# A hybrid decoder layer with dense experts: more blocks of first expert products between and ahead of the top-16 selection, the one-hot stage and the second products

## The chip, the cores and the metric

One core of one Trainium2 chip runs the whole layer. The metric is device microseconds of one execution of the program; lower is better. The engines are named as the profile names them: PE (TensorE matmul), PEld (its weight loads), DVE (VectorE), ACT (ScalarE), POOL (GpSimd), SP (SyncE, which here only issues DMAs). Matrix operands are split into a rounded part and a remainder ("hi" and "lo") and multiplied in three passes.

## The reference

```python
h2  = modulate(rms_norm(x, norm2_g), shift2, scale2)      # after conv, attention and w_out
q   = (h2 @ w_peer_q).reshape(T, 8, 2, 128)
s1, s2 = q[:, :, 0] @ keys1.T, q[:, :, 1] @ keys2.T        # 8 heads, 128 + 128 keys
v1, i1 = top_k(s1, 16);  v2, i2 = top_k(s2, 16)
cand   = v1[..., :, None] + v2[..., None, :]               # 256 sums, index i1 * 128 + i2
top_s, top_p = top_k(cand, 16);  g = softmax(top_s)
a = einsum('thkd,td->thk', expert_u[idx], h2)              # 16384 experts of one neuron
w = gelu(a) * g
ffn = einsum('thk,thkd->td', w, expert_v[idx])
x = x + gate2 * ffn
```

There are 512 tokens, 2048 features, 128 x 128 experts, all float32.

## The kernel before

The front part (modulation, projections, attention, output projection, query projection `w_peer_q`) is not touched. The expert part treats two groups of tokens differently. The first TG = 160 tokens gather their chosen experts' rows by indirect DMA on POOL's queue and combine them on DVE (`gather_u`, `gather_v`: 320 gathers of 1 MB in 323 steps). The other TD = 352 tokens are done densely: every expert is multiplied with every token, and a table of gates, zero for experts that were not chosen, picks out the result.

The dense part runs over NK = 128 blocks of 128 experts. A **first product** (`u_block(e)`) is 48 matmuls of 352 columns into a PSUM tile `pa`. Its weights come as 1 MB `ur` from `u_dram`; each half of a block is turned by a DVE transpose (blocks 12 and up), split by ACT (hi) and by DVE (lo, `ut<-ur,ut`, in `split`) into `ut`, of which there are two buffers, so that the split of half n + 1 can stand ahead of the matmuls of half n. GELU writes the result to a tile of `GE`. `w_block(e)` multiplies a pair of results with the gates `g` from `g_dram` and splits them into a `W` tile (five buffers). A **second product** (`v_group(ch, dg)`) is 96 matmuls over a chunk of CH = 8 blocks, with weights `vr` split into `vs`; sixteen chunks of four groups. `u_dram` is the first expert matrix laid out in blocks, by copies from DRAM to DRAM (`lay_out`, four DMAs of 256 KB per block, on SP's queue, 116 blocks in all) that are spread over the whole front part.

Between the query projection and the chunks stand two stages. The **last selection**: for each of the four tiles of 128 tokens `select(i, 3, ...)` does the top-16 work of the last two heads, nearly all on DVE (`top16`; `tkj` compares on DVE, multiplies on POOL, reduces on DVE to `idxf`), and `finish_select` the softmax and the transposes of indices and gates (`fi`, `opT`). The **one-hot stage**: in 11 rounds of 32 tokens, four steps each, DVE writes one-hot rows (`gt<-iof,opT`, 128x2048), POOL and ACT scale them to `og`, PE multiplies them (`pv<-og,gt`, 8 matmuls a step), ACT collects `gtile`, and a DMA stores 2 MB of gates to `g_dram`. The first gates can be loaded only after the last store has landed.

RUN = 12 first products are done ahead of the chunks: four before the four tiles of the last selection, eight after the last eight one-hot rounds. Their results wait in two W tiles (blocks 0 to 7) and in `gacc` (8 to 11), an accumulator that the gathers of the second kind need later.

Every engine runs its instructions in program order; the order is made by a scheduler from the order of the code, the data and the extra orderings that the code adds (`add_manual_dep` with ORDER). SP's DMAs are issued in its program order too. The steps of the gathers are tied to `pace`, a list of matmuls.

## Time and profile before

| | |
|---|---|
| median of 3 runs | 3346.73 us (3344.19 to 3349.19) |
| profiled execution | 3349.88 us, of which 3347.6 us span |
| mean granted TensorE clock | 0.978 of full speed |
| PE busy | 3176.0 us, 95% of the span |
| DVE busy | 2739.1 us, 82% |
| ACT, POOL busy | 1223.3 us (37%), 1057.7 us (32%) |
| DMA | 1017.81 MB, 304 GB/s on the mean |

The expert part begins near 1180 us with the first of the 48 x 128 first-product matmuls; the last selection lies between 1185 and 1257 us, the one-hot stage between 1264 and 1400 us, and the second products begin at 1416 us. From there to 3250 us the chunks run, and the last 100 us add the gathered part and store the output. A row of the trace gives the start or a count, then the busy time, and in brackets or behind the bar the idle time ahead of it and what ended it.

### The profile page before, as it was taken

Reading aid. Unit: us, or ns where it says so; the run is one execution under the profiler, and the core shown is the slowest. Engines: PE = TensorE matmul, PEld = TensorE weight load, DVE = VectorE, ACT = ScalarE, POOL = GpSimd, SP = SyncE. Lnnn points to the kernel's source line nnn. Section 1 sums busy time; section 2 is a strip of 40 time slices with the busy share of each in tenths; the row PEclk is TensorE's granted clock in tenths of the full one; section 3 lists DMA queues with packets and bytes.
Section 4 is the critical chain, followed back from the end, with each engine's and each line's share of the span. In section 5 each row is a group of like instructions: output and inputs, shape, how many; then the busy total and the mean of one; then the engine's idle time right before and its main releaser. Section 6 shows DMA issues by size and latency. Waiting matters only on the chain.

```text
span 3347.6 us, 47029 instructions
## 1 busy us (share of the span) xinstructions
PE 3176.0 (95%) x18006; PEld 2945.2 (88%) x18006; DVE 2739.1 (82%) x3631; ACT 1223.3 (37%) x1866; POOL 1057.7 (32%) x709
## 2 busy tenths in 40 slices
PE   5889999999999859999999999999999999999998
PEld 4777877777777659999999999999999999999997
DVE  6888477842338998789999899999999999999975
ACT  5246343343255336632333333333333333333322
POOL 2447333353435634312222232222222222222210
PEclk9999999999999979999999999999999999999998
DMA  9878978966979878989989899998988898999964
GB/s 303 283 257 294 345 250 280 299 211 221 315 256 302 261 243 288 335 290 364 343 332 343 310 333 363 325 338 323 340 333 316 336 354 329 360 330 338 338 222 158
DMA packets 388896, 1017.81 MB, mean 304 GB/s; under 512 B 29713, under 2 KB 108478, under 8 KB 328126
## 3 DMA queue, kind: packets, MB, share of 16 engines
q1 hardware_dynamic: 342590, 679.23, 59.8%
q0 software_dynamic: 46080, 335.56, 25.7%
q8 instruction: 141, 2.31, 0.3%
q14 instruction: 85, 0.70, 0.1%
HBM read 965.11 MB, written 171.18 MB: 339 GB/s over the span
## 4 chain that ended last, share of the span: by engine, by line
PE 55%; DVE 4%; issue 2%; DMA 1%; ACT 0%; POOL 0%; DVEq 0%; ACTq 0%; SPq 0%; POOLq 0%
PE pa L835 26%; PE pv L1004 26%; PE pv L974 2%; DVE gacc L910 1%; DVE ut L90 1%; DMA xs<-x_dram 1%; DVE gt L963 1%; DVE ur L823 1%; DVE vs L90 1%; DMA gt<-in_expert_v_dram,idxu 0%; DMA gt<-in_expert_u_dram,idxu 0%; ACT ut L89 0%; DVE acc L1020 0%; PE pv L1061 0%; DVE gt L897 0%
## 5 line engine op out<-in xcount | busy, mean ns | idle before, releaser
L835 PE MATMUL pa<-hd,ut 128*128 128x352 f32 x6144 | 1067.2, 326 | 37.5 <-DVE ut L90 23.6
L1004 PE MATMUL pv<-W,vs 128*128 128x352 f32 x6144 | 1052.1, 325 | 5.1 <-ACT W L89 2.6
L835 PEld LDWEIGHTS pa<-hd,ut 128*128 128x128 f32 x6144 | 1010.9, 190 | 42.4 <-DVE ut L90 26.6
L1004 PEld LDWEIGHTS pv<-W,vs 128*128 128x128 f32 x6144 | 1001.8, 189 | 8.0 <-ACT W L89 3.5
L90 POOL TENSOR_TENSOR wsp<-wraw,wsp 128x1024 fp32r<-128x1024 f32 x160 | 389.0, 2434 | 557.6 <-ACT wsp L89 525.4
L89 ACT ACTIVATE vs<-vr 128x1024 fp32r<-128x1024 f32 x256 | 271.6, 1061 | 737.9 <-PE pv L1004 687.8
L89 ACT ACTIVATE ut<-ur 128x1024 fp32r<-128x1024 f32 x256 | 269.6, 1056 | 315.2 <-PE pa L835 239.5
L897 DVE SCALAR_TENSOR_TENSOR gt<-gt,h2n 128x2048 f32<-128x2048 f32 x160 | 364.6, 2283 | 18.3 <-DMA gt<-in_expert_u_dram,idxu 18.3
L910 DVE SCALAR_TENSOR_TENSOR gacc<-gt,ga_a,gacc 128x2048 f32<-128x2048 f32 x158 | 369.9, 2341 | 6.8 <-DMA gt<-in_expert_v_dram,idxu 6.7
L889 POOL DMA_INDIRECT gt<-in_expert_u_dram,idxu x128 | 183.0, 1430 | 554.6 <-DVE gt L897 320.8
L90 DVE TENSOR_TENSOR vs<-vr,vs 128x1024 fp32r<-128x1024 f32 x256 | 311.2, 1216 | 57.3 <-ACT vs L89 56.9
L90 DVE TENSOR_TENSOR ut<-ur,ut 128x1024 fp32r<-128x1024 f32 x256 | 310.9, 1219 | 55.6 <-ACT ut L89 54.4
L889 POOL DMA_INDIRECT gt<-in_expert_v_dram,idxu x128 | 172.4, 1347 | 552.3 <-DVE gacc L910 360.1
L89 ACT ACTIVATE wsp<-wraw 128x1024 fp32r<-128x1024 f32 x160 | 169.2, 1058 | 346.5 <-issue 72.0
L507 PE MATMUL pm<-big,wsp 128*128 128x512 f32 x1152 | 285.2, 401 | 0.0
L823 DVE STREAM_TRANSPOSE ur<-ur 128x1024 f32<-128x1024 f32 x232 | 274.5, 1221 | 0.1
L507 PEld LDWEIGHTS pm<-big,wsp 128*128 128x128 f32 x1152 | 214.9, 191 | 42.6
L282 PE MATMUL pqk<-wsp,big 128*128 128x512 f32 x768 | 190.1, 407 | 18.0 <-DVE qk L334 13.6
L748 PE MATMUL pm<-big,wsp 128*128 128x512 f32 x768 | 188.5, 403 | 19.0 <-POOL wsp L90 17.4
L282 PEld LDWEIGHTS pqk<-wsp,big 128*128 128x128 f32 x768 | 148.7, 196 | 53.0 <-DVE qk L334 17.0
L748 PEld LDWEIGHTS pm<-big,wsp 128*128 128x128 f32 x768 | 147.2, 195 | 52.2 <-POOL wsp L90 20.0
L593 PE MATMUL pm<-big,wsp 128*128 128x512 f32 x768 | 182.1, 397 | 6.2 <-DVE x L599 6.2
(274 smaller groups left out, 3024.0 us busy)
## 6 DMA issues: line engine op xcount, KB each, us to landing
ur<-u_dram SPq DMA_DIRECT2D x128, 1024.0 KB, 7.8
vr<-in_expert_v_dram SPq DMA_DIRECT2D x256, 512.0 KB, 7.2
u_dram<-in_expert_u_dram SPq DMA_DIRECT2D x464, 256.0 KB, 6.7
ada_w<-in_w_ada_dram SPq DMA_DIRECT2D x192, 512.0 KB, 5.5
wraw<-in_w_in_dram SPq DMA_DIRECT2D x96, 512.0 KB, 5.7
g_dram<-gtile SPq DMA_DIRECT2D x11, 2048.0 KB, 7.4
g<-g_dram SPq DMA_DIRECT2D x32, 704.0 KB, 9.4
wraw<-in_w_out_dram SPq DMA_DIRECT2D x32, 512.0 KB, 5.5
```

Source lines behind the costliest of these rows:

```text
L89: hi = nc.scalar.activation(dst[:, 0], src, AF.Copy)
L90: (eng or nc.vector).tensor_tensor(out=dst[:, 1], in0=src, in1=dst[:, 0].bitcast(F32), op=OP.subtract)
L282: nc.tensor.matmul(banks[i], hT[kk][:, a, i * P:(i + 1) * P], ws[:, b, k], start=(kk == last[0] and n == 0), stop=(kk == last[1] and n == 2))
L507: nc.tensor.matmul(banks[n2], ws[:, a, k, n2 * P:(n2 + 1) * P], hT[kk][:, b], start=(kk == 0 and n == 0), stop=(kk == KC - 1 and n == 2))
L593: nc.tensor.matmul(banks[j], ws[:, a, k, j * P:(j + 1) * P], yT[kk0 + k][:, b], start=(kq == 0 and k == 0 and n == 0), stop=(kq == 7 and k ...
L748: nc.tensor.matmul(banks[j], ws[:, a, k, j * P:(j + 1) * P], h2T[kk][:, b], start=(kk == 0 and n == 0), stop=(kk == KC - 1 and n == 2))
L823: nc.vector.transpose(t, t)
L835: mm = nc.tensor.matmul(pa[:, :TD], ut[:, a, j].rearrange("p b r -> p (b r)"), hd[k][:, b], start=(k == 0 and n == 0), stop=(k == KC - 1 a ...
L889: d = nc.gpsimd.indirect_dma_start(out=t, out_offset=None, in_=src, in_offset=bass.IndirectOffsetOnAxis(ap=gidx[g][:, j:j + 1], axis=0))
L897: return lambda: nc.vector.scalar_tensor_tensor(t, t, 1.0, h2n, op0=OP.mult, op1=OP.mult, accum_out=ga_a[:, j:j + 1])
L910: return lambda: nc.vector.scalar_tensor_tensor(gacc, t, a, gacc, op0=OP.mult, op1=OP.add)
L1004: mm = nc.tensor.matmul(pv[j // 2][:, j % 2, :TD], vs[:, a, bb, j * P:(j + 1) * P], W[e0 // 2][:, m, bb], start=(b == 0 and n == 0), stop= ...
```

## The change

The change moves work in time and adds a detour by DRAM; no product, selection or gather is added or dropped.

- RUN becomes 16. `u_block` becomes a generator of halves (`u_halves`), so that `u_half(upto)` can do one half (24 matmuls) at a time.
- In the last selection `select` calls `between()` after each of its portions; `one_more` there does one half of a block and ties the next portion's first DVE instruction behind that half's lo split (`after[0] = split.lo`). Ten blocks (RUN_TK) are done so, where before there were four.
- The other six go into the one-hot stage, spread over its steps.
- Results 12 to 15 do not fit on chip: two pairs go to `ge_dram` and come back into W tiles in `w_block`.
- Blocks 16 and 17 are coded ahead of the first chunk.
- `lay_out` is called for 3 blocks instead of 4 per tile of the selection, and in the one-hot stage for one block in rounds 0 to 5 and two in rounds 6 to 10 (before: one, and two in round 7).
- The steps of the gathers are spread by a count of units done (`gather_by`: 1 for a quarter of a second-product group, 0.61 for a quarter of a first product) instead of by the block's number.

```diff
...
-RUN_MAX = 12
+RUN = 16
+LAY_TK = 3
+RUN_TK = 10
+U_PART = 0.61
...
+        split.lo = (eng or nc.vector).tensor_tensor(out=dst[:, 1], in0=src, in1=dst[:, 0].bitcast(F32),
+                                                    op=OP.subtract)
...
+        ge_dram = tc.dram_tile([RUN // 2, P, 2, TD], F32, name="ge_dram")
...
+        after = [None]
+
         def top16(v, ix, s, tmp):
-            nc.vector.max(out=v[:, 0:8], in_=s)
+            t = nc.vector.max(out=v[:, 0:8], in_=s)
+            if after[0] is not None:
+                tc.add_manual_dep(t.ins, after[0].ins.name, ORDER, reason="products in turn with the selection")
+                after[0] = None
...
-        def select(i, hp, s):
+        def select(i, hp, s, between=lambda: None):
             v = tk.tile([P, 2, 2, 16], F32, name="tkv")
             ix = tk.tile([P, 2, 2, 16], U32, name="tki")
             for h in range(2):
                 for m in range(2):
                     tmp = tk.tile([P, P], F32, name="tkt")
                     top16(v[:, h, m], ix[:, h, m], s[:, h, m], tmp)
+                between()
...
+        NKEPT = NGE + D // (2 * TD) * 2
...
-        def u_block(e, behind=None):
+        def u_halves(e):
             pa = psA.tile([P, T], F32, name="pa")
             for q in range(2):
                 u_turn(e * 2 + q + AHEAD)
...
                     for n, (a, b) in enumerate(PASSES):
                         mm = nc.tensor.matmul(pa[:, :TD], ut[:, a, j].rearrange("p b r -> p (b r)"), hd[k][:, b],
                                               start=(k == 0 and n == 0), stop=(k == KC - 1 and n == 2))
-                        if behind is not None:
-                            tc.add_manual_dep(mm.ins, behind.ins.name, ORDER, reason="work left for the turn")
-                            behind = None
                     if e >= RUN and j % 4 == 3:
                         pace.append(mm)
-                        gather_to(e // CH * CH + (e % CH + (q * 2 + j // 4 + 1) / 4) * 0.55)
+                        gather_by(U_PART)
+                if q == 0:
+                    yield mm
             if e % 2 == 0:
                 if e < NGE:
                     if e % 4 == 0:
                         gts[0] = wpool.tile([P, 2, 2, TD], F32, name="W")
                     GE[e // 2] = gts[0][:, e // 2 % 2]
+                elif e < NKEPT:
+                    GE[e // 2] = gacc[:, (e - NGE) * TD:(e - NGE + 2) * TD].rearrange("p (i t) -> p i t", i=2)
                 elif e < RUN:
-                    GE[e // 2] = gacc[:, (e - NGE) * TD:(e - NGE + 2) * TD].rearrange("p (i t) -> p i t", i=2)
+                    GE[e // 2] = spill[0].tile([P, 2, TD], F32, name="ges", bufs=2)
                 else:
                     GE[e // 2] = up.tile([P, 2, TD], F32, name="ge", bufs=GE_BUFS)
             nc.scalar.activation(GE[e // 2][:, e % 2], pa[:, :TD], AF.Gelu)
-            return mm
+            if NKEPT <= e < RUN and e % 2:
+                nc.sync.dma_start(ge_dram[e // 2], GE.pop(e // 2))
+            yield mm
+
+        def u_block(e):
+            for _ in u_halves(e):
+                pass
+
+        spill = [None]
+        ahead_of = itertools.chain.from_iterable(u_halves(e) for e in range(RUN))
+        halves = [0]
+
+        def u_half(upto):
+            while halves[0] < upto:
+                u_half.mm = next(ahead_of)
+                halves[0] += 1
...
+            if e % 2 == 0 and NKEPT <= e < RUN:
+                if (e - NKEPT) % 4 == 0:
+                    gts[0] = wpool.tile([P, 2, 2, TD], F32, name="W")
+                GE[e // 2] = gts[0][:, e // 2 % 2]
+                nc.sync.dma_start(GE[e // 2], ge_dram[e // 2])
...
+        def one_more():
+            if halves[0] < 2 * RUN_TK:
+                u_half(halves[0] + 1)
+                after[0] = split.lo
+
         for i in range(NT):
-            mm = u_block(i)
-            lay_out(4, mm)
-            select(i, 3, held[i])
+            one_more()
+            lay_out(LAY_TK, u_half.mm)
+            select(i, 3, held[i], one_more)
             finish_select(i)
+        u_half(2 * RUN_TK)
...
-        def gather_to(blocks):
-            first = 0.55 * CH
-            frac = min(1.0, max(0.0, (blocks - first) / (NK - first - CH)))
+        n_units = (NK // CH - 1) * 4 * (CH // 2) + (NK - CH - RUN) * 4 * U_PART
+        units = [0.0]
+
+        def gather_by(n):
+            units[0] += n
+            frac = min(1.0, units[0] / n_units)
...
+                    done_ = (b * GB + t8 + 8) / TD
+                    u_half(2 * RUN_TK + round(2 * (RUN - RUN_TK) * done_))
                 nc.sync.dma_start(g_dram[b], gt_)
-                lay_out(min(1 + (b % 8 == 7), len(lay)), gm)
-                if b >= nb_ - (RUN - NT):
-                    u_block(RUN - nb_ + b, behind=gm if b == nb_ - 1 else None)
-
+                lay_out(min(1 + (b > 5), len(lay)), gm)
+
+        assert halves[0] == 2 * RUN
...
-                gather_to(ch * CH + CH * 0.55 + (dg * (CH // 2) + b2 + 1) * 0.225)
+                gather_by(1.0)
...
+        for e in range(RUN, RUN + 2):
+            u_block(e)
         for ch in range(nch):
             for b in range(CH):
                 e = ch * CH + b
-                if e >= RUN:
+                if e >= RUN + 2:
                     u_block(e)
                 w_block(e)
             if ch == nch - 1:
                 up_ctx.close()
                 fin = ctx.enter_context(tc.tile_pool(name="fin", bufs=2))
-                gather_to(NK)
+                gather_by(n_units)
...
```

In the programs as built, the scheduler moves first products further forward than the code says. PE has 266 first-product matmuls ahead of its first one-hot matmul before, and 652 in the change; ahead of its first second-product matmul (`pv<-W,vs`) 626 before, and 960 (20 blocks) in the change. DVE's lo splits from the start of the last selection are 10 before the last tile's `fi` and 26 in the change; 24 up to the last one-hot instruction before, and 42 in the change, with 4 and 22 transposes.

On DVE, at the end of a tile's selection in the middle of the stage (`tkj` are the compares that POOL's multiplication follows, `cv` the candidate sums of the next tile, `ut` the lo split, `idxf` the reduction that needs POOL's result); before:

```order
L723 TENSOR_TENSOR tkj<-iot,tkpf 128x864 x2
L710 TENSOR_TENSOR cv<-tkv 128x2x8
L710 TENSOR_TENSOR cv<-tkv 128x2x10
L710 TENSOR_TENSOR cv<-tkv 128x2x12
L90 TENSOR_TENSOR ut<-ur,ut 128x1024
L702 TENSOR_SCALAR tkf<-tki 128x2x16
```

and in the change, for the second of the four tiles:

```order
L736 TENSOR_TENSOR tkj<-iot,tkpf 128x864 x2
L94 TENSOR_TENSOR ut<-ur,ut 128x1024
L786 COPY gmx<-gate_7535 128x8
L739 TENSOR_REDUCE idxf_7531<-tkj 128x16
L790 TENSOR_TENSOR gate_7535<-gate_7535,gmx 128x128
L739 TENSOR_REDUCE idxf_7531<-tkj 128x16
L94 TENSOR_TENSOR ut<-ur,ut 128x1024
```

A lo split now follows the compares directly and another follows the tile's last reduction, where before the next tile's sums stood.

On PE, at the first second-product matmul (`pa` are first products, `pv<-og,gt` the one-hot products); before:

```order
L835 MATMUL pa<-hd_7552,ut 128x352 x3
L835 MATMUL pa<-hd_7553,ut 128x352 x3
L835 MATMUL pa<-hd_7538,ut 128x352 x2
L1004 MATMUL pv<-W,vs 128x352 x2
L835 MATMUL pa<-hd_7538,ut 128x352
```

and in the change:

```order
L852 MATMUL pa<-hd_7552,ut 128x352
L852 MATMUL pa<-hd_7553,ut 128x352 x3
L852 MATMUL pa<-hd_7554,ut 128x352 x3
L1022 MATMUL pv<-og,gt 128x128 x112
L1053 MATMUL pv<-W,vs 128x352 x460
L852 MATMUL pa<-hd_7539,ut 128x352 x3
```

Before, 98 first-product matmuls stand between the last one-hot product and the first second product and more follow it; in the change none stands between, and 460 second-product matmuls follow in one run.

On SP, at the end of the one-hot stage (the store of the gates, the copies of `lay_out`, then the first load of gates `g`); before:

```order
L249 DMA u_dram<-in_expert_u_dram 128x1x512 x4
L976 DMA g_dram<-gtile 128x4096
L863 DMA g_11862<-g_dram 128x11x128
L994 DMA vr<-in_expert_v_dram 128x2x512 x3
L820 DMA ur<-u_dram 128x2048
```

and in the change:

```order
L255 DMA u_dram<-in_expert_u_dram 128x1x512 x8
L1026 DMA g_dram<-gtile 128x4096
L255 DMA u_dram<-in_expert_u_dram 128x1x512 x3
L901 DMA g_12238<-g_dram 128x11x128
L1043 DMA vr<-in_expert_v_dram 128x2x512 x3
```

Eight copies instead of four now stand ahead of the last store of gates, and three behind it, ahead of the first load.

## Rows read from the trace of the kernel before

**Rows 1.** The page: busy us (share of the span) and instructions of two engines.

```profile
PE 3176.0 (95%) x18006; PEld 2945.2 (88%) x18006; DVE 2739.1 (82%) x3631; ACT 1223.3 (37%) x1866; POOL 1057.7 (32%) x709
```

**Rows 2.** Busy time by stage: us, engines' busy us (instructions), granted clock, DMA share, GB/s.

```profile
1180.00:1262.60 82.60, 48.18 (x230) 45.36 (x228) 75.39 (x290) 22.72 (x28) 26.52 (x30) 0.75 0.79 247
1262.60:1369.70 107.10, 107.08 (x822) 106.89 (x820) 92.58 (x49) 72.03 (x152) 49.87 (x34) 1.00 0.81 295
1369.70:1400.00 30.30, 24.56 (x193) 22.46 (x194) 26.62 (x14) 21.01 (x48) 17.68 (x12) 1.00 0.96 368
...
1416.00:3250.00 1834.00, 1825.22 (x11301) 1821.29 (x11300) 1714.29 (x1427) 580.45 (x650) 444.34 (x320) 1.00 0.90 332
```

**Rows 3.** Groups of PE instructions, 1165 to 1263 us: the first products.

```profile
L835 PE MATMUL pa<-hd,ut 128*128 128x352 f32 x223 | 47.9, 381 | 30.8 <-DVE ut L90 19.4 <-ACT ut L89 11.3
```

**Rows 4.** PE in order of time, last selection: start us, us, instruction, idle before.

```profile
1179.64 0.59 PE L835 MATMUL pa<-hd,ut 128*128 128x352 f32 x2 [1.53 <-ACT ut L89]
1190.30 14.62 PE L835 MATMUL pa<-hd,ut 128*128 128x352 f32 x72 [10.07 <-DVE ut L90]
```

**Rows 5.** Busy time of a window inside the chunks, with PE full.

```profile
1700.00:1750.00 50.00, 50.00 (x312) 50.00 (x312) 45.34 (x43) 16.30 (x19) 13.16 (x9) 1.00 0.85 318
```

**Rows 6.** DVE in order of time, last selection: its first and last instruction, and between.

```profile
1184.76 0.86 DVE L688 MAX8 tkv<-gt 128x8 f32<-128x128 f32 x4
...
1204.33 3.74 DVE L710 TENSOR_TENSOR cv<-tkv 128x16 f32<-128x16 f32 x3
1207.99 1.21 DVE L90 TENSOR_TENSOR ut<-ur,ut 128x1024 fp32r<-128x1024 f32 x1
...
1257.04 0.29 DVE L785 CAST fi<-iu 128x256 f32<-128x256 uint32 x1
```

**Rows 7.** DVE in order of time, the tail of the one-hot stage.

```profile
1368.68 1.21 DVE L90 TENSOR_TENSOR ut<-ur,ut 128x1024 fp32r<-128x1024 f32 x1
1369.80 15.47 DVE L963 TENSOR_TENSOR gt<-iof,opT 128x2048 f32<-128x2048 f32 x7
1385.19 2.36 DVE L823 STREAM_TRANSPOSE ur<-ur 128x1024 f32<-128x1024 f32 x2
1387.47 8.85 DVE L963 TENSOR_TENSOR gt<-iof,opT 128x2048 f32<-128x2048 f32 x4
```

**Rows 8.** PE in order of time, one-hot stage (16 matmuls make 32 records).

```profile
1270.09 3.73 PE L974 MATMUL pv<-og,gt 128*128 128x128 f32 x32
1273.58 3.15 PE L835 MATMUL pa<-hd,ut 128*128 128x352 f32 x18
```

**Rows 9.** Groups of DVE instructions, 1262 to 1402 us.

```profile
L963 DVE TENSOR_TENSOR gt<-iof,opT 128x2048 f32<-128x2048 f32 x44 | 98.7, 2283 | 11.0 <-PE pv L974 10.8 <-issue 0.2
L90 DVE TENSOR_TENSOR ut<-ur,ut 128x1024 fp32r<-128x1024 f32 x14 | 17.1, 1220 | 8.8 <-ACT ut L89 8.4
```

**Rows 10.** All engines in order of time, from the one-hot stage to the second products.

```profile
1399.82 16.07 PE L835 MATMUL pa<-hd,ut 128*128 128x352 f32 x98
...
1400.72 0.33 SPq L976 DMA_DIRECT2D g_dram<-gtile  x1
...
1407.67 0.38 SPq L863 DMA_DIRECT2D g<-g_dram  x1
...
1412.56 1.70 DVE L868 TENSOR_TENSOR W<-W,g 128x704 f32<-128x704 f32 x2 [2.04 <-DMA g<-g_dram]
...
1415.73 0.48 PE L1004 MATMUL pv<-W,vs 128*128 128x352 f32 x2
...
1416.11 1.22 DVE L90 TENSOR_TENSOR vs<-vr,vs 128x1024 fp32r<-128x1024 f32 x1
```

**Rows 11.** SP's queue in order of time: copies of `lay_out` issued in the last selection.

```profile
1192.57 26.90 SPq L249 DMA_DIRECT2D u_dram<-in_expert_u_dram  x32
```

**Rows 12.** Waits, 1220 to 1260 us: us in total, times, longest.

```profile
ACT ut L89 <- DMA ur<-u_dram: 5.7, 1, 5.7
```

More of the change, by code (lines that the diff above doesn't have):

```diff
@@ L1 @@
+import itertools
 import math
@@ L89, in split @@
         hi = nc.scalar.activation(dst[:, 0], src, AF.Copy)
-        (eng or nc.vector).tensor_tensor(out=dst[:, 1], in0=src, in1=dst[:, 0].bitcast(F32), op=OP.subtract)
+        split.lo = (eng or nc.vector).tensor_tensor(out=dst[:, 1], in0=src, in1=dst[:, 0].bitcast(F32),
+                                                    op=OP.subtract)
         return hi
@@ L714, in select @@
                 o += n
+            between()
             for h in range(2):
@@ L726, in select @@
                 nc.vector.tensor_reduce(idxf[i][:, hh * 16:hh * 16 + 16], eq, axis=AX.X, op=OP.add)
+                between()
         def scores(qs, i, sp, s):
@@ L771, in finish_select @@
             mx = tk.tile([P, 8], F32, name="gmx")
-            nc.vector.tensor_copy(mx, gv[:, :, 0])
+            t = nc.vector.tensor_copy(mx, gv[:, :, 0])
+            if after[0] is not None:
+                tc.add_manual_dep(t.ins, after[0].ins.name, ORDER, reason="products in turn with the selection")
+                after[0] = None
             nc.vector.tensor_tensor(out=gv, in0=gv, in1=mx[:, :, None].to_broadcast([P, 8, 16]), op=OP.subtract)
@@ L810, in hymba_peer @@
         gacc = gp.tile([P, D], F32, name="gacc")
-        RUN = min(NGE + D // TD, RUN_MAX)
+        NKEPT = NGE + D // (2 * TD) * 2
         gts = {}
@@ L956, in hymba_peer @@
             nb_ = TD // GB
+            spill[0] = gs
             for b in range(nb_):
```

## The prediction, made before the run

> **What bounds the kernel now.** I read the page first. PE is busy 95% of the span and DVE 82% [rows 1], so time can only be won where PE stands idle or runs at a low clock. Busy time by stage shows where that is [rows 2]. In the chunks PE is busy 1825.2 of 1834.0 us: almost nothing is left there. In the middle of the one-hot stage it is busy 107.08 of 107.10 us. In the last selection it is busy 48.2 of 82.6 us, at a mean granted clock of 0.75, while DVE is busy 75.4: this stage is DVE's. In the tail of the one-hot stage PE loses 5.7 of 30.3 us.
>
> The groups of PE instructions say what it waits for in the selection: 30.8 us of idle time ahead of the first products, for the lo split on DVE and the hi split on ACT [rows 3]. The rows in order of time show the effect on the clock. After 10.07 us of idling, 72 matmuls take 14.62 us, or 0.203 us each [rows 4]; with PE full it is 50/312 = 0.160 us [rows 5]. That stretch therefore costs (0.203 - 0.160) x 72 = 3.1 us besides the idling, the clock being partly on the lower of its two levels.
>
> **What PE loses before, from 1179.6 us to the first second product at 1415.7 us** [rows 4, 10]. By the built order 626 first-product matmuls and 352 one-hot matmuls lie in it. A first-product matmul takes 0.160 us; 16 one-hot ones take 1273.58 - 1270.09 = 3.49 us, or 0.218 each [rows 8]. That is 100.2 + 76.7 = 176.9 us, with 1 us of transposes (an estimate) 178, of 236: 58 us are lost. This is all that can be won here.
>
> **What the change moves.** 960 instead of 626 matmuls stand ahead of the first second product. The 334 that no longer come behind it are worth 334 x 0.160 = 53.4 us of a stage in which PE is full. So the time changes by how much later the second products start, minus 53.4 us.
>
> PE's sum up to the last one-hot product: 960 x 0.160 + 352 x 0.218 + 1 = 231.4 us. The first lo split now stands behind four selection instructions that take 0.86 us from 1184.76 [rows 6]; with 1.2 us for itself PE starts near 1187. PE alone would be through at 1418.4 us.
>
> DVE's sum. The selection of the four tiles ran from 1184.76 to 1257.3 us, with ten lo splits in it [rows 6]. A lo split costs 1369.80 - 1368.68 = 1.12 us from start to start, two transposes 2.28, a one-hot instruction 15.39/7 = 2.2 [rows 7]. The selection alone is 72.6 - 11.2 = 61.4 us. Now: 61.4 + 42 lo splits (47.0) + 22 transposes (25.1) + 44 one-hots (96.8) = 230.3 us, which ends at 1415.1. Before, the last one-hot instruction ended at 1396.3 and PE turned from the one-hot products at 1399.8 [rows 7, 10], 3.5 us later. DVE alone would be through at 1418.6 us.
>
> So two engines that feed each other each need the whole time. Work that is equal on both sides and coupled through two `ut` buffers does not run without gaps: a lo split that waits for PE holds up the selection behind it, and a late one holds up PE. From below this costs nothing: PE was full for 107 us in the one-hot stage, but there DVE had slack. What DVE lost there behind PE is the nearest row: 11.0 + 8.8 us of idling [rows 9], less 5.6 that fell ahead of the first one-hot instruction, 14.2 us. I take 14.2 and 25 (14.2 plus 11 for a second such stretch) as the upper end. The last one-hot product then ends at 1432.7 us.
>
> On DVE each tile's two `tkj` compares are now followed by a lo split. Before, sums `cv` stood there that took 3.74 us for three while POOL multiplied, and a lo split behind them took 1.21 as always [rows 6]. The held instructions are in the 61.4 us already; what moves is who is held. The Trainium skill (SBUF — State Buffer, Who interferes with whom) says that a DVE instruction with two SBUF inputs and a GpSimd one that reads SBUF share an exclusive port, and that the later one waits for the whole of the other. The trace agrees, with 3.74 us for those three. By the rule the lo split would be held about 1.9 us per tile and the sum for DVE would stay, with PE waiting up to 4 x 1.9 = 7.6 us more; that is inside the 14.2.
>
> **The junction.** Before, the last gates are stored at 1400.72, loaded from 1407.67, multiplied at 1412.56, and the first second product starts at 1415.73; its third pass needs a lo split that starts at 1416.11 and is done 1.12 us later, at 1417.2 [rows 7, 10]. All this time PE worked on 98 first-product matmuls. In the change none stand there: blocks 16 to 19 were pulled ahead of the last one-hot products. The PSUM tiles are then full, since results 18 and 19 wait for a place. So PE idles 1417.2 - 1399.8 = 17.4 us, and pays 3.1 us of low clock, as after the 10 us of idling in [rows 4]. From below the clock costs nothing; from above, the store of the gates is late: eight copies instead of four stand ahead of it, and up to three gathers of 1 MB start there. DMA was 0.96 busy at 368 GB/s in this tail [rows 2]; one more MB of copies and one of gathers ahead of it make 2.1/0.368 = 5.7 us, which is the upper end.
>
> Sum: full pace at 1432.7 + 17.4 + 3.1 = 1453.2 us, against 1415.7 before: 37.5 us later, minus 53.4, makes -15.9 us.
>
> **What costs nothing.** The detour of four results moves 4 x 0.36 MB, 1.4/0.332 = 4.3 us of DMA spread over a stage that is 0.90 busy [rows 2]; without that cover it would be 4.3 us. The copies are 28 blocks in these two stages before and after. The gathers now have 53 us less of PE time to hide in: DVE is busy 1714.3 of 1834.0 us in the chunks, 93.5%; minus 37 us of splits and transposes that move ahead (16 x 1.12 + 18 x 1.14 = 38), over 1781 us, it is 94.1%. I take zero for this, with 8 us either way: PE's idling in the chunks, 8.8 us [rows 2], may go or double.
>
> The profiled execution took 3349.9 us, 3.2 above the median of 3346.7. -15.9 us gives 3334 for it and 3331 for the median. A measurement here tells about 0.2% (6.7 us) from no change.
>
> **Rivals.**
>
> - *The two engines interlock without loss.* For it: PE at 107.08 of 107.10 us. Against it: DVE had slack there, and now none. It gives -15.9 - 14.2 = -30, or 3317. Chance 0.14.
> - *The junction grows and the coupling is at its upper end*: -15.9 + 10.8 + 5.7 = +0.6, 3347, no change. For it: DMA at 0.96 with more copies ahead of the store. Against it: the copies are issued some 10 us ahead. Chance 0.22. The Trainium skill (DMA: Bandwidth & Descriptors, Issuing engines are not separate DMA queues) has DMAs of different engines run on the same DMA engines and interleave, so the gathers on POOL's queue would slow the store on SP's; no row of before has the two together here.
> - *Rows `ur` come late behind the copies of the selection* (the slower side). Twelve copies in one run stand ahead of a `ur` load once per tile; 32 took 26.9 us [rows 11], so twelve take 10 us, more than the 7.7 us that PE needs for the block in hand. One such wait was 5.7 us on ACT [rows 12]. With four, and the selection standing behind the split in DVE's order, it is 22.8 us: -15.9 + 22.8 = +7, 3354. It decides from 4.0 us a tile. Against it: the copies in this stage fall from 16 blocks to 12 (while its `ur` loads rise to some 14), and DMA is only 0.79 busy there [rows 2]. Chance 0.13.
> - The likeliest, 3331, from 3320 to 3340: 0.51.
>
> Faster by over 0.2%: 0.65; within: 0.22; slower: 0.13. The range takes in the lossless case and stops between no change and the slower case: 3313 to 3350.
>
> **What would show it.** PE's busy time in the selection should rise from 48 to over 85%, and DVE's should stay full, until about 1290 us. The last one-hot product should end at 1433 us (1419 to 1444). Between it and the first second product PE should be idle for 16 to 23 us, with the load of the gates at the end of the wait, and the rows behind it should be at the lower clock for some microseconds. Behind it PE should be full as before. The prediction is wrong if the scheduler's order lets PE wait long within the selection (lo splits late, or `ur`), or if the one-hot stage is longer than DVE's sum by over 25 us.

## The result and the profile after

| | before | changed kernel |
|---|---|---|
| median | 3347.93 us (6 runs, 3339.32 to 3350.7) | 3372.74 us (6 runs, 3367.44 to 3384.46) |
| profiled execution, span | 3349.88, 3347.6 us | 3384.46, 3382.6 us |
| first product to first second product | 236.1 us | 305.3 us |
| from there to the end | 1931.9 us | 1890.1 us |

The ratio is 1.0082, 95% interval 1.0062 to 1.0102: slower by 0.8%, where 0.5% faster was forecast; 3372.74 lies outside the range. The profiled execution is 12 us above its median, and its front part, which the change doesn't touch, is 7.6 us longer than in the profile before (first product at 1187.2 us instead of 1179.6). Stages are therefore compared from the first product on: 69.2 us later at the second products, 41.8 us shorter behind them, 27.4 us in all, which agrees with the ratio (0.0082 x 3347.93 = 27.5).

The page of the changed kernel, which answers to [rows 1]:

```profile
PE 3184.5 (94%) x18006; PEld 2952.2 (87%) x18006; DVE 2749.1 (81%) x3631; ACT 1226.1 (36%) x1868; POOL 1064.3 (31%) x709
```

The work is the same; the shares fell because the span grew. The windows by stage, to be read beside [rows 2]: selection, one-hot stage, junction (last one-hot product to first second product), first 100 us of the second products, chunks, last 150 us (columns: us, then PE, PEld, DVE, ACT, POOL busy, granted clock, DMA share, GB/s):

```profile
1187.20:1314.70 127.50, 110.66 (x646) 107.58 (x647) 104.94 (x314) 47.94 (x58) 30.04 (x31) 0.95 0.61 209
1314.70:1461.40 146.70, 136.35 (x1028) 133.03 (x1027) 133.72 (x76) 92.21 (x194) 72.28 (x46) 0.99 0.81 301
1461.40:1492.50 31.10, 0.33 (x4) 0.14 (x2) 7.23 (x8) 2.46 (x5) 1.88 (x2) 0.54 0.96 370
1492.50:1592.50 100.00, 95.42 (x560) 93.34 (x561) 80.08 (x78) 30.89 (x34) 18.49 (x14) 0.95 0.86 301
1592.50:3232.60 1640.10, 1640.10 (x10184) 1639.56 (x10183) 1538.53 (x1278) 520.55 (x584) 406.58 (x288) 1.00 0.90 333
3232.60:3382.60 150.00, 120.42 (x684) 115.08 (x682) 105.64 (x153) 35.14 (x67) 16.89 (x14) 0.87 0.63 230
```

PE is filled to 87% in the selection, as meant. But DVE, which was to stay full there, is busy 104.94 of 127.50 us, the junction is 31 us of idle PE, and the last 150 us are worse than before, where the same window reads:

```profile
3197.60:3347.60 150.00, 132.43 (x784) 127.32 (x782) 91.03 (x152) 40.98 (x74) 7.23 (x4) 0.93 0.49 175
```

**The selection.** The waits between 1187 and 1315 us (who waited for whom: us in total, times, longest):

```profile
ACT ut L93 <- PE pa L852: 35.3, 10, 11.7
...
DVE ut L94 <- ACT ut L93: 20.0, 11, 3.2
...
ACT W L870 <- PE pa L852: 19.7, 7, 3.1
...
PE pa L852 <- DVE ut L94: 16.7, 8, 6.7
```

This is a ring: PE waits for DVE's lo split, DVE for ACT's hi split, ACT for PE. Both PE and DVE lose 17 to 20 us in one stage. DVE in order of time, end of one tile's selection (start, us, instruction, idle before it):

```profile
1206.70 1.23 DVE L94 TENSOR_TENSOR ut<-ur,ut 128x1024 fp32r<-128x1024 f32 x1 [1.85 <-ACT ut L93]
1208.77 1.23 DVE L94 TENSOR_TENSOR ut<-ur,ut 128x1024 fp32r<-128x1024 f32 x1 [0.85 <-ACT ut L93]
1209.92 0.21 DVE L696 MAX8 gate<-cv 128x8 f32<-128x54 f32 x1
1213.28 1.23 DVE L94 TENSOR_TENSOR ut<-ur,ut 128x1024 fp32r<-128x1024 f32 x1 [3.16 <-ACT ut L93]
...
1218.05 2.90 DVE L94 TENSOR_TENSOR ut<-ur,ut 128x1024 fp32r<-128x1024 f32 x1
1220.88 1.84 DVE L786 COPY gmx<-gate 128x8 f32<-128x8 f32 x1
```

From 1206.70 to 1214.4 DVE does three lo splits and one MAX8 of 0.21 us; the selection stands behind splits that can't run yet. What the third waited for shows on ACT:

```profile
1211.84 0.47 ACT L870 ACTIVATE W<-pa 128x352 f32<-128x352 f32 x1 [3.10 <-PE pa L852]
1212.20 1.05 ACT L93 ACTIVATE ut<-ur 128x1024 fp32r<-128x1024 f32 x1
```

The hi split stands behind the GELU of a block that PE had still to finish. At 1218.05 a split takes 2.90 us instead of 1.21 and the COPY behind it 1.84, beside POOL's two multiplies:

```profile
1217.31 5.38 POOL L738 TENSOR_TENSOR tkj<-tkj,ci 128x864 f32<-128x864 f32 x2 [11.42 <-DVE tkj L736]
```

That is the held split of the prediction, 1.7 us longer where it allowed 1.9; the COPY behind it ends with the second multiply, at 1222.7 us. The rule cited in the prediction from the Trainium skill (SBUF — State Buffer, Who interferes with whom), an exclusive port for a DVE instruction with two SBUF inputs and a GpSimd one that reads SBUF, agrees with the split's row. DVE's groups in the stage give the sum (busy us, mean ns of one):

```profile
L94 DVE TENSOR_TENSOR ut<-ur,ut 128x1024 fp32r<-128x1024 f32 x27 | 39.6, 1469 | 20.0 <-ACT ut L93 20.0
...
L786 DVE COPY gmx<-gate 128x8 f32<-128x8 f32 x4 | 5.7, 1424 | 0.0
```

27 splits at 1.21 and four COPYs at 0.16 would take 33.3 us; 12.0 us of DVE's time went into being held. Most of that isn't new. Before, the held ones were the sums `cv`, which take 3.4 us in the changed kernel, and two conversions `tkf` (4.8 us instead of 1.4), some 10 us in all:

```profile
L710 DVE TENSOR_TENSOR cv<-tkv 128x16 f32<-128x16 f32 (+3 forms) x20 | 9.5, 504 | 0.0
```

What is new is the waiting, 20.0 us for the hi split where the ten splits before waited 0.0.

**The junction**, all engines in order of time, to be read beside [rows 10]:

```profile
1454.59 10.02 SPq L255 DMA_DIRECT2D u_dram<-in_expert_u_dram  x8
...
1456.97 1.12 POOL L933 DMA_INDIRECT gt<-in_expert_u_dram,idxu  x1 [1.04 <-PE pv L1022]
...
1461.74 0.60 ACT L1023 ACTIVATE gtile<-pv 128x512 f32<-128x512 f32 x1 [0.29 <-PE pv L1022]
1462.50 0.94 POOL L933 DMA_INDIRECT gt<-in_expert_u_dram,idxu  x1 [1.77 <-ACT gtile L1023]
1467.35 0.33 SPq L1026 DMA_DIRECT2D g_dram<-gtile  x1
...
1469.97 0.94 POOL L933 DMA_INDIRECT gt<-in_expert_u_dram,idxu  x1 [6.53 <-DVE gt L941]
1470.44 3.71 SPq L255 DMA_DIRECT2D u_dram<-in_expert_u_dram  x3
...
1483.53 0.38 SPq L901 DMA_DIRECT2D g<-g_dram  x1
...
1489.76 1.69 DVE L906 TENSOR_TENSOR W<-W,g 128x704 f32<-128x704 f32 x2 [16.96 <-DMA g<-g_dram]
1490.69 0.79 ACT L93 ACTIVATE W<-W 128x704 fp32r<-128x704 f32 x1 [28.35 <-DVE W L906]
1491.38 1.04 ACT L93 ACTIVATE vs<-vr 128x1024 fp32r<-128x1024 f32 x1
```

The last `gtile` is complete at 1462.3, but SP issues eight copies until 1464.6, waits 2.7 us for one of them to land, and issues the store only at 1467.35; the load that needs it follows 16.2 us later (7.0 before), among three more copies and four gathers. Before, no gather stood in the junction: the first one started 8 us behind the first second product.

```profile
1423.90 1.35 POOL L889 DMA_INDIRECT gt<-in_expert_u_dram,idxu  x1 [25.94 <-PE pv L1004]
```

PE in order of time behind the junction of the changed kernel; its row names the weights `vr`, but their hi split stands on ACT behind that of W, which waited for the gates:

```profile
1492.48 15.08 PE L1053 MATMUL pv<-W,vs 128*128 128x352 f32 x76 [30.77 <-DMA vr<-in_expert_v_dram]
```

76 matmuls at 0.198 us instead of 0.160 cost 2.9 us: the low clock after idling (granted 0.50 from 1480 to 1496 us and 1.00 from 1500 on), forecast at 3.1.

### The profile page after: what moved, and what is told of

Same layout as the page of the kernel before. It is cut to its first block, busy times and chain, and to the rows that moved or that the text cites. A ratio compares the mean times of both kernels' runs of the same rounds, so it can differ in the third digit from the quotient of the medians.

```text
span 3382.6 us, 47053 instructions
## 1 busy us (share of the span) xinstructions
PE 3184.5 (94%) x18006; PEld 2952.2 (87%) x18006; DVE 2749.1 (81%) x3631; ACT 1226.1 (36%) x1868; POOL 1064.3 (31%) x709
## 4 chain that ended last, share of the span: by engine, by line
PE 71%; DVE 13%; DMA 11%; issue 2%; POOL 1%; ACT 1%; SPq 1%; DVEq 0%; ACTq 0%; POOLq 0%
PE pa L852 27%; PE pv L1053 27%; PE pm L513 6%; PE pm L599 4%; DMA ada_w<-in_w_ada_dram 4%; DMA u_dram<-in_expert_u_dram 2%; PE pm L288 2%; DVE run L221 1%; PE pv L1022 1%; PE sp L467 1%; DVE ada_acc L221 1%; DVE ut L94 1%; DMA vr<-in_expert_v_dram 1%; DMA xs<-x_dram 1%; PE pqk L288 1%
## 5 line engine op out<-in xcount | busy, mean ns | idle before, releaser
L852 PE MATMUL pa<-hd,ut 128*128 128x352 f32 x6144 | 1057.7, 325 | 19.2 <-DVE ut L94 16.7
L94 DVE TENSOR_TENSOR ut<-ur,ut 128x1024 fp32r<-128x1024 f32 x256 | 319.3, 1251 | 47.2 <-ACT ut L93 45.7
L288 PEld LDWEIGHTS pqk<-wsp,big 128*128 128x128 f32 x768 | 149.7, 198 | 54.1 <-DVE qk L340 17.8
```

Source lines behind the costliest of these rows:

```text
L94: split.lo = (eng or nc.vector).tensor_tensor(out=dst[:, 1], in0=src, in1=dst[:, 0].bitcast(F32), op=OP.subtract)
L288: nc.tensor.matmul(banks[i], hT[kk][:, a, i * P:(i + 1) * P], ws[:, b, k], start=(kk == last[0] and n == 0), stop=(kk == last[1] and n == 2))
L852: mm = nc.tensor.matmul(pa[:, :TD], ut[:, a, j].rearrange("p b r -> p (b r)"), hd[k][:, b], start=(k == 0 and n == 0), stop=(k == KC - 1 a ...
```

## The experiments

All fifteen, by stage, each from its profiled execution (us; "to W" is first product to first second product). These single executions differ from their medians by some microseconds, the changed kernel's (11.7 above) and e1's (10.4 below) most; the ratios, against the kernel before on the same chip, come from the timed runs.

| kernel | ratio (95%) | selection | one-hot | junction | to W | rest |
|---|---|---|---|---|---|---|
| before | 1 | 84.5 | 135.7 | 15.9 | 236.1 | 1931.9 |
| changed | 1.0082 (1.0062 to 1.0102) | 127.5 | 146.7 | 31.1 | 305.3 | 1890.1 |
| e1 | 1.0081 (1.0064 to 1.0098) | 131.7 | 147.7 | 22.8 | 302.2 | 1879.0 |
| e2 | 1.0074 (1.0058 to 1.0091) | 126.8 | 121.6 | 46.0 | 294.4 | 1894.7 |
| e3 | 1.0063 (1.0047 to 1.0080) | 130.8 | 124.7 | 29.0 | 284.5 | 1898.3 |
| e4 | 1.0043 (1.0026 to 1.0060) | 88.4 | 136.8 | 31.6 | 256.8 | 1916.7 |
| e5 | 1.0030 (1.0015 to 1.0045) | 104.9 | 151.6 | 33.0 | 289.5 | 1885.4 |
| e6 | 1.0006 (0.9988 to 1.0024) | 113.7 | 132.2 | 36.1 | 282.0 | 1891.0 |
| e7 | 1.0023 (1.0007 to 1.0039) | 84.4 | 162.7 | 29.7 | 276.8 | 1900.1 |
| e8 | 1.0024 (1.0008 to 1.0040) | 84.0 | 135.7 | 15.9 | 235.6 | 1932.0 |
| e9 | 1.0067 (1.0046 to 1.0088) | 127.3 | 144.5 | 24.9 | 296.7 | 1898.9 |
| e10 | 0.9988 (0.9976 to 1.0000) | 105.7 | 134.3 | 21.9 | 261.9 | 1899.8 |
| e11 | 1.0007 (0.9993 to 1.0021) | 105.7 | 152.4 | 15.5 | 273.6 | 1895.7 |
| e12 | 0.9985 (0.9971 to 0.9999) | 105.9 | 134.1 | 31.8 | 271.8 | 1890.5 |
| e13 | 1.0048 (1.0029 to 1.0067) | 107.1 | 152.1 | 32.4 | 291.6 | 1885.2 |
| e14 | 1.0019 (1.0005 to 1.0032) | 106.2 | 116.7 | 21.9 | 244.8 | 1926.7 |
| e15 | 0.9981 (0.9970 to 0.9993) | 104.9 | 124.1 | 24.8 | 253.8 | 1903.8 |

**e1: the copies laid out as before.**

```diff
-LAY_TK = 3
+LAY_TK = 4
-                lay_out(min(1 + (b > 5), len(lay)), gm)
+                lay_out(min(1 + (b % 8 == 7), len(lay)), gm)
```

> The change, with the copies of lay_out as before (four blocks per tile of the last selection; one per one-hot round and two in round 7), so that 4 instead of 8 copies stand ahead of the last store of gates and none instead of 3 behind it. Theory A (the copies hold up the last store and the first load of gates, while the rest of the junction is as predicted): the stretch from the last one-hot product to the first second product falls from 31 us to 16 to 19 us and the time by about 13 us, to some 3360. Theory B (the junction is long because no first product is left to fill it, whatever the copies do): it stays over 27 us and the time within 4 us of 3373. Theory C (the selection's portions are unequal and DVE waits for PE within them): no change of the 15 us that DVE waits ahead of its lo splits in the selection; with a third more copies there it could grow by some 3 us.

The store is issued right after the last `gtile` and the junction shrinks by 8.3 us, but the selection grows by 4.2 and the ratio doesn't move. What theory A alone wins is less than the intervals (some 9 us together) can tell.

**e2: block 16 held behind the last one-hot product**, so that PE has work at the junction; its first matmul gets

```diff
+                        if behind is not None:
+                            tc.add_manual_dep(mm.ins, behind.ins.name, ORDER, reason="work left for the turn")
```

> The change, with the first matmul of block 16 ordered behind the last one-hot product, as the kernel before did with its last block: 192 first-product matmuls (30.7 us) then stand between the last one-hot product and the first second product, and 192 fewer among the one-hot products. Theory B: PE is busy for 30 us of the junction, the one-hot stage is some 18 us shorter (16 splits and transposes less on DVE), and the time falls by 15 to 25 us, to 3350 to 3358. Theory A: the gates arrive as late as now after the last one-hot product (28 us), but that costs nothing any more because PE has work. Theory C: the selection is as long as now (115 us on DVE), and so the time stays above that of the kernel before by 5 to 10 us.

33 us of work now stand in the junction, and the one-hot stage is 25 us shorter, but the junction grows to 46 us: the store is issued 7.8 us after the last product, and the load follows 17.8 us later. The ratio falls by 0.0008 where 15 to 25 us were expected. **e3: both.**

> Both edits of the two runs above together. If both A and B hold as separate costs, the time falls by 25 to 31 us, to 3342 to 3348, level with the kernel before; if they are one cost seen twice (a filled junction needs no early gates), it is within 4 us of the run with the hold alone.

PE is now busy 24.4 of 29 us there, and still three quarters of the loss remains. A and B are true of the junction and small in the time of the changed kernel.

**e4: the kernel before with the changed kernel's layout of copies** (`LAY_TK` and the `lay_out` line of e1, the other way round).

> The kernel before, with the copies of lay_out late as in the change (three blocks per tile of the selection, two per round from round 6): 8 and 11 copies ahead of the last two stores of gates. Theory A alone: the first gates come 10 us or more later than before (they came 12.7 us after the last one-hot product) and the time rises by 8 to 14 us. Theory B (a cover of first products decides): the gates come later, but 178 first-product matmuls (28 us) stand between, so the time stays within 4 us of the kernel before.

It costs 0.43%, some 14 us as theory A alone had it, although first products cover the junction (29.4 of 31.6 us): the second products start 20.7 us later after the first product, and the rest gives only 15.2 of that back.

**e5: five portions a tile**, none behind the candidate sums.

```diff
                 o += n
-            between()
```

> The changed kernel with five portions of selection a tile instead of six: no half block behind the candidate sums, which are a portion of only 1 to 2 us. Twenty halves then spread over all four tiles; before, they were used up after three and a third. Theory C (portions of unequal length make DVE's lo splits wait for PE, 15 to 20 us in this stage): from the first product to the first one-hot instruction 127 us becomes 113 to 119, and the time falls by 8 to 14 us. Theory D (what costs is the ring itself: PE's products, ACT's GELU and hi split, DVE's lo split wait for one another in two buffers, however the selection is cut): the stage stays at 122 to 128 us, the time within 5 us of the changed kernel. Theory A or B (only the junction matters): no change either.

This is the largest single mend: the ratio falls by 0.0052 (17 us), and so do selection and one-hot stage together (274.2 to 256.5 us). **e6: the mends of e1, e2 and e5 together.**

> All three mends together: copies laid out as before, block 16 held behind the last one-hot product, five portions a tile. If the parts add up (theory C): junction covered (24 of 29 us busy, as in e3_both), selection near 116 us, from the first product to the second products 268 to 274 us, the time 10 us below e3_both, near 3355, and with that still 8 to 11 us above the kernel before. By theory D the selection stays at 125 to 131 us and the time at 3362 to 3368. By my recorded sum (coupling 14 us, no loss at the junction) it would be 3320 to 3330.

The sum of the parts arrives (some 19 us below e3, where 10 were expected), with no measurable difference from before. What is new is in the selection: ACT's hi split has 17.6 us of waits that end with copies to `u_dram`, with four blocks of copies a tile in SP's queue instead of three.

**e7: e3 with the selection as before the change**, four whole blocks, the other twelve in the one-hot stage.

```diff
-RUN_TK = 10
+RUN_TK = 4
-            one_more()
+            u_half(2 * (i + 1))
-            select(i, 3, held[i], one_more)
+            select(i, 3, held[i])
```

> As e3_both, but the selection is left as it was before the change: four whole blocks, one ahead of each tile, none between portions; the other twelve blocks ahead of time go into the one-hot stage. If the halves between portions win what they should (PE's idling in the selection, 34 us before), undoing them costs it: the stage is 85 us long, PE idles 30 to 35 us in it, the one-hot stage is PE-full and 160 to 170 us long, and the time is 10 to 25 us above e3_both. If they win nothing (theory D: each half costs DVE about as long as PE gains), pa to second products is 275 to 290 us as in e3_both (284.5) and the time within 6 us of it, or below.

The one-hot stage is full, with DVE busy 136.92 us, and the time is 13 us (0.0040) below e3:

```profile
1265.60:1428.30 162.70, 162.70 (x1228) 162.70 (x1227) 136.92 (x79) 101.28 (x208) 70.75 (x44) 1.00 0.76 280
```

So the halves between portions, six a tile, cost more than they won. Five a tile (e6) are 0.0017 below e7, but the intervals overlap.

**e8: the kernel before with the gathers spread by units** (`gather_by`).

> The kernel before with one thing of the change: the gathers' steps spread by units done instead of by the block's number. The changed kernel has PE full in the chunks where the one before lost 9 us. Theory E (the spread is what filled them): PE's busy share in the chunks 100%, the time 6 to 10 us below before. Rival (PE is full there because the gathers had more work ahead of them, or because the splits moved ahead): no change, within 4 us.

No gain, but 0.24% slower: theory E falls. The prediction had no term for this part of the change. Where the 8 us go isn't shown: the stages of the profiled execution are those of before. Nor was the changed kernel run with the old spread.

**e9: the changed kernel without gathers in front of the second products.**

```diff
-                        gather_by(U_PART)
+                        gather_by(U_PART if e >= RUN + 2 else 0)
```

> The changed kernel with one thing altered: blocks 16 and 17 no longer count as units for the gathers, so that no gather stands in front of the second products; before the change the first one started 8 us behind them, in the changed kernel four (4 MB) started from 5 us ahead of the last one-hot product on. Theory F (the gathers in POOL's queue take DMA from the store and the load of the gates at the junction): from the last one-hot product to the first second product 31 us becomes 18 to 23, and the time falls by 6 to 12 us, to a ratio of 1.005 to 1.006. Rival (the eleven copies are what slows the store, theory A, or the chain of small steps does): 28 to 31 us, no change in time.

The junction shrinks by 6.2 us, but the rest grows by 8.8, most of it in the last 150 us, where PE is busy for 113.8 us instead of 120.4, and 4.1 in the first 100 us of second products. What is won early is lost late, and the time hardly moves.

```profile
3224.20:3374.20 150.00, 113.84 (x663) 108.32 (x661) 107.38 (x153) 34.56 (x66) 19.40 (x16) 0.88 0.63 235
```

**e10 to e12: five portions a tile, copies early** (three blocks a tile, then two in rounds 0 to 4: `1 + (b < 5)`), with and without the hold and the late gathers.

> Five portions a tile, block 16 held behind the last one-hot product, gathers late as in e9, and copies neither in the selection's way nor at the end: three blocks a tile as in the changed kernel, two in rounds 0 to 4 of the one-hot stage and one in rounds 5 to 10. If the causes found so far are all (C, B, A, F): selection 103 to 107 us (as in e5), one-hot 120 to 130, junction 18 to 25 with 15 or more busy, from the first product to the second products 245 to 258 us, the rest 1895 to 1900 us, and the time 10 to 20 us below before, a ratio of 0.994 to 0.997. If what remains is theory D (the ring costs about what it wins): within 0.2% of before, like e6_all.

> As e10, without holding block 16 behind the last one-hot product. Theory B (work for PE at the junction is worth its length): the junction is 18 to 23 us with PE idle, the one-hot stage 15 to 25 us longer, and the time 5 to 12 us above e10. Rival (held work only moves: what the junction covers, the one-hot stage or the chunks lose): within 4 us of e10.

> As e10, with the gathers as early as in the changed kernel. Theory F: junction 33 to 38 us as in e6_all, part of it uncovered, and one long run of second products with waits behind it; the time 6 to 12 us above e10. Against e6_all it differs only in where the copies stand: if copies late in the selection hold up the rows ur (13.7 us of waits there in e6_all), the selection is 103 to 107 us instead of 113.7 and the time 4 to 9 us below e6_all; if not, equal.

e10 is 4 us faster than before, at the edge of its interval, where 10 to 20 were expected. Without the hold (e11) the ratio is 0.0019 higher, about 6 us, with intervals that overlap a little; the way to W is 11.7 us longer, as expected. Late or early gathers make no difference (e10, e12). The copies shorten the selection, 105.9 us in e12 instead of 113.7 in e6; the time is 0.0021 lower, with intervals that overlap. The junction of e11 shows the bare chain, store to load 6.3 us and 15.5 in all:

```profile
1435.41 0.33 SPq L1025 DMA_DIRECT2D g_dram<-gtile  x1
1441.73 0.37 SPq L900 DMA_DIRECT2D g<-g_dram  x1
...
1434.50:1450.00 15.50, 0.25 (x3) 0.06 (x1) 2.59 (x3) 2.35 (x4) 0.00 (x0) 0.62 0.76 282
```

**e13: five halves a tile, but the short portion kept** (the one left out is that ahead of tiles 1 to 3).

```diff
+            if i == 0:
+                one_more()
-            one_more()
```

> The changed kernel with five halves a tile as in e5, but the one left out is that ahead of the tile instead of that behind the candidate sums: the short portion stays, and the twenty halves still reach all four tiles (578 first products ahead of the first one-hot product, as in e5). Theory C as stated (unequal portions): the two halves around the short portion still wait, the selection stays at 116 to 127 us, and the time at 3362 to 3372 us, ratio 1.005 to 1.008. Rival (the halves were used up after three and a third tiles, so that the rest of the selection ran as before with PE waiting; five a tile mends it whichever is left out): 103 to 108 us, ratio 1.002 to 1.004 as in e5.

The stage is 107.1 us, as the rival said, so unequal portions are not the main thing; the ratio, 1.0048, lies between the two forecasts. The waits between 1183 and 1290 us, beside those of the changed kernel above:

```profile
PE pa L852 <- DVE ut L94: 11.3, 8, 6.7
DVE ut L94 <- ACT ut L93: 8.0, 7, 2.8
```

Both engines wait less at once. e5, whose interval overlaps that of e13, differs from it in what POOL holds up; its COPYs, not behind POOL's multiplies, take

```profile
L94 DVE TENSOR_TENSOR ut<-ur,ut 128x1024 fp32r<-128x1024 f32 x24 | 32.6, 1361 | 6.9 <-ACT ut L93 6.9
...
L785 DVE COPY gmx<-gate 128x8 f32<-128x8 f32 x4 | 0.6, 158 | 0.0
```

so that its splits and COPYs are held for 3.6 us (32.6 - 24 x 1.21), those of e13 for 8.4 and those of the changed kernel for 12.0.

**e14 and e15: e10 with 12 and with 14 blocks ahead** (`RUN`).

> As e10, with 12 blocks ahead of time instead of 16 (ten in the selection, two in the one-hot stage; no detour by DRAM), so that blocks 13 and up stay to be done among the first second products. Theory G (the second products at the start of the chunks run at full pace only where first products stand among them: before, 624 matmuls in the first 100 us, in every kernel with 16 blocks 534 to 581): 615 to 624 matmuls in the first 100 us, from the first product to the second products 238 to 248 us, and the time 4 to 10 us below e10, a ratio of 0.996 to 0.998. Rival (the loss there is due to DMA or to the gates, whatever stands among them): 560 to 580 matmuls, and the time 5 to 15 us above e10, since 192 first products less are done ahead.

> As e14 with 14 blocks ahead of time. If the number of blocks matters by what stays for the chunks (theory G): between e10 and e14, 600 to 624 matmuls in the first 100 us, from the first product to the second products 245 to 255 us, ratio 0.995 to 0.998. If only the sum of products done ahead counts: as e10 (0.9988) within 3 us.

Neither filled the first 100 us, so theory G falls. e14 is 0.31% (10 us) above e10, as the rival said; e15 is as e10 within 3 us, as its second forecast said. At 0.2% below before e15 is the fastest by its median, with an interval that overlaps those of e10 and e12, and its last 150 us are as full as before:

```profile
1429.40:1529.40 100.00, 94.34 (x571) 92.99 (x571) 81.53 (x80) 31.19 (x33) 17.90 (x14) 0.98 0.85 296
3183.20:3333.20 150.00, 134.31 (x831) 129.63 (x829) 111.05 (x162) 42.29 (x76) 15.53 (x11) 0.98 0.65 232
```

## Why the prediction was wrong, step by step

**PE's sum held, the coupling did not: the main failure.** First product to last one-hot product took 274.2 us. The prediction's own terms for it are 7.4 us until PE starts (1187 - 1179.6), 231.4 of work and 14.2 of coupling, 253.0; so the coupling measured 35.4 us, above its upper end of 25. PE was full from 1330 to 1420 us; it lost time in the selection and in the tail of the one-hot stage, where no first products were left and DVE's one-hot rows came late. DVE was late by its waits: 20.0 us for the hi split in the selection, where e5 has 6.9 and e13 8.0. The term was sized from [rows 9], where DVE lost 14 us with slack to spare. Here six halves a tile take 6 x 24 x 0.160 = 23.0 us of PE, and a quarter of the selection with six lo splits 15.4 + 6.7 = 22.1 us of DVE: neither can make up what it lost to the other. With five it is 19.2 to 21.0, and selection and one-hot stage shrink by 17.7 us (e5) and 15.0 us (e13), so that the coupling is 17.7 and 20.4. That fewer halves a tile nearly halve it is shown; that the near-equality is why is argued. For it speaks e7, whose one-hot stage is full with DVE busy 84% of it. The rival that stays is that five a tile also carry the twenty halves to the last tile, where six are used up early.

**The junction, 17.4 us, measured 31.1.** Mechanism and bare chain were right (15.5 us in e11), and so was the clock. The upper end took 5.7 us more for copies and gathers together; they cost 14.2: in the changed kernel 5.0 us by SP, which issues the copies ahead of the store, and 9.2 us by the store's slow landing (16.2 instead of 7.0). Taking the copies away (e1) gave 8.3 us back, the gathers (e9) 6.2. From store to load it took 16.2 us among copies and gathers and 10.4 without the gathers (e9). The Trainium skill (DMA: Bandwidth & Descriptors, Issuing engines are not separate DMA queues) has DMAs that different engines issue run on the same DMA engines and interleave, and these times agree with it.

**-53.4 us behind the first second product measured -41.8**, or -44.7 without the 2.9 us of clock. "The gathers now have 53 us less of PE time to hide in", taken at zero, should have been a cost. Behind the first second product PE stands idle for 34.2 us instead of 26.4: 4.6 instead of none in the first 100 us, none instead of 8.8 in the chunks (1640.10 of 1640.10 us), 29.6 instead of 17.6 in the last 150. There PE does 12.0 us less than before, while DVE has 105.6 us of work instead of 91.0; the last gather starts 88.0 us before the end instead of 126.5:

```profile
3294.61 1.19 POOL L933 DMA_INDIRECT gt<-in_expert_v_dram,ib  x1 [3.37 <-DVE gacc L954]
```

and before, of 3347.6 us:

```profile
3221.14 0.94 POOL L889 DMA_INDIRECT gt<-in_expert_v_dram,ib  x1 [8.60 <-PE pv L1004]
```

That the late gathers are why is argued. For it speak e9, e10 and e11, which delay them: PE is busy for 112.9 to 113.8 us in the last 150. Against it speaks e15, whose last gather starts 90.9 us before the end and whose end is full. e15 and e14 lose 11 us in their chunks instead. So the loss moves between the end and the chunks with the number of blocks, and what places it stays open.

**The sum.** (35.4 - 14.2) + (31.1 - 17.4) = 34.9, and the rest 8.5 worse than -53.4 + 3.1 = -50.3: -15.9 + 43.4 = +27.5 us, and 27.4 were measured. The three terms are read off the same execution, so that they add up shows only that nothing is left out.

**The rivals.** "The junction grows and the coupling is at its upper end" named what happened, but both went past their ends. `ur` late behind copies did not happen in the selection (1.4 us of waits on DVE), and did in e6, with four blocks of copies a tile. The held split was as forecast. That what moves is only who is held, the sum for DVE staying, held within some 2 us: 12.0 us of splits and COPYs against some 10 of sums and conversions before, which are in the 61.4 us. Of the forecast signs, PE over 85% busy in the selection, the load of the gates ending the wait, and the low clock behind it came true; a full DVE, the end of the one-hot products at 1433 us (1461.4, of which 7.6 are the longer front part), 16 to 23 us of idle PE behind it (31) and a full PE behind the junction did not.

**Open.** Why the first 100 us of second products lose 3 to 9 us of PE's time in all other kernels, where before they were full: most of PE's waits there end with the split of `vs`. The new spread alone (e8) loses 3.1 us there, late copies alone (e4) 6.2, and first products standing among them (e14, e15) did not mend it. Open too is how much of the 0.24% of e8 is in the loss of the changed kernel, and what the detour of four results costs, which e14 lacks but no run isolates.

## What to carry to other kernels

Two engines that feed each other through two buffers should not both be planned to 100%: leave one of them some tenth of slack (here five halves a tile, 19.2 of 21.0 us, cost 18 to 20 us where six cost 35), and size the coupling from a stage with as little slack as the planned one. Work pulled forward has a second price where it stood, namely the time in which something else was hidden: look who is at 94% there. A transfer on the critical chain should be the first thing its queue issues, with bulk copies and gathers placed where nothing waits for them.

## What the runs showed of the hardware

- One store of 2 MB took from 6.3 us (e11) over 10.4 (copies, e9) and 13.7 (gathers, e1) to 16.2 us (both) until the load behind it could be issued, in junctions with 282 to 374 GB/s of traffic: with other transfers, on its own queue and on POOL's, it took more than twice as long.
- A DVE COPY of 128x8 elements took 1.84 us once, beside POOL's multiply, and 1.42 on the mean of four in the changed kernel, 0.16 in e5: besides the split with two inputs, a small one-input instruction was held as well.
